# RWKV-7's block transfers between SBUF and DRAM scratch, issued from SP's queue

## The chip, the cores and the metric

One core of a Trainium2 chip runs the whole program. The metric is the device time of one execution in microseconds (us). The engines are named as in the profile: PE (TensorE), DVE (VectorE), ACT (ScalarE), POOL (GpSimd) and SP (SyncE). Any of ACT, POOL and SP can issue a DMA: the issue is an instruction in that engine's own program, and an engine runs its program in the order in which the framework's scheduler wrote it when the kernel was built.

## The reference

Two layers of a streaming-encoder trunk act on 512 frames of width 1024, all in fp32. Layer 0 normalises its input, projects it, and splits the columns between two mixers: HGRN2 (four heads, H0 to H3) and RWKV-7 (eight heads of width 64). Their outputs, ya and yb, are joined, projected by one output matrix, and added to x. A SwiGLU feed-forward block follows. Layer 1 does the same with S5 and mLSTM as mixers. A last normalisation closes it.

The part that matters here is RWKV-7's recurrence, which the reference runs frame by frame:

```python
def step(state, inp):
    r_t, w_t, k_t, v_t, a_t, b_t = inp
    sa = jnp.einsum("bhvk,bhk->bhv", state, a_t)
    state = (state * w_t[:, :, None, :] + sa[..., None] * b_t[:, :, None, :]
             + v_t[..., None] * k_t[:, :, None, :])
    return state, jnp.einsum("bhvk,bhk->bhv", state, r_t)
```

## The kernel before, in words

**Weights.** Every large product is made of three passes: weight and activation are each split into a high and a low part, and high by high, high by low and low by high are added up in PSUM. The weights stream in from DRAM one block after the other. `wissue` (L340) issues one block's load from SP into a tile `raw`, of which there are two. ACT casts it to `hi` (L375) and DVE or POOL subtracts to get `lo` (L376), 256 columns at a time. The rings of `hi` and `lo` hold two blocks, and the load of a block is written one block ahead of its use. PE's matmuls all stand at L292, and their results for dense products go to two PSUM tiles `d`. Small copies that any engine may do stand at L281, element by element products at L277, activations at L253.

**RWKV-7 by chunks.** The kernel takes 64 frames as a chunk, so that the recurrence becomes products of matrices and one triangular system for each chunk and head. Heads go in pairs P0 to P3, the sequence in two halves g = 0 and 1. One group (q, g) is two pairs and one half, so there are four groups. For each group there are three kinds of work:

- `rwp(q, g)`: gates and then `rw_prep` for both pairs. It builds the triangular matrix A in the tile `pb`. Its diagonal blocks of 32 by 32 are then written to DRAM scratch `scr_a`, with four DMAs for a pair (L952).
- `inv(q, g)`: `rw_inverse`, on POOL alone. It loads the blocks of both pairs back as `iw` and `iu` with one block to a partition (eight DMAs, L987 and L988), inverts them all at once in 30 steps (L992, L994), and stores the result to `scr_u` (four DMAs, L1000).
- `rwd(q, g)`: `rw_solve` for both pairs loads the inverted blocks into `ub` with four DMAs for a pair (L1010) and does four products with it. Then `rw_chain` carries the state through the four chunks: ACT and DVE copy a PSUM result to `sb` (L281), PE transposes it (L1059), and for pairs P0 and P1 SP stores the output to `scr_yb` (L1090).

There are 32 such DMAs at L952 in all and 32 at L1010, of 16 KB each.

**What sets the order.** The dense work F runs through the projections in the order L, P0, P1, H0, P2, P3, H1, H2, H3. A table, `prog`, weaves F with RWKV-7's groups: each stage takes F up to one label while it runs one or two group steps beside it. The last two stages are `inv(1,0)` and `rwp(1,1)` beside F up to H3, and `inv(1,1)` with `rwd(1,0)`. A head of HGRN2 (`hgrn`) ends with a store of its output `y` to `scr_ya` from SP (L837). After the last stage the pool of HGRN2's tiles is closed. `xtiles` (L520) then loads eight tiles x of the residual, 256 KB each, from ACT's queue, into memory that this pool held. `outa` reloads ya and yb as `yraw` from SP (L1174), splits them, multiplies five of the eight row blocks by the weights wO0a, and lets DVE add the PSUM result to x (L1183). It is woven with `rwd(1,1)`.

The scheduler weaves the program by its own estimate of when an instruction can start, so the order on every engine can shift when one instruction's engine is changed.

**The table that the change touches.** `dq(j)` gives the queue for each of four kinds of DMA:

```python
def dq(j):
    return {"s": nc.sync, "g": G, "a": S}[PRM["dq"][j]]

dq(0).dma_start(scr_a[...], pb[...])    # L952, in rw_prep
dq(1).dma_start(iw[w], ...)             # L987, and iu at L988, in rw_inverse
dq(2).dma_start(scr_u[...], iw[w])      # L1000, in rw_inverse
dq(3).dma_start(ub[...], scr_u[...])    # L1010, in rw_solve
```

In it `S` is ACT's queue (nc.scalar), `G` is POOL's (nc.gpsimd) and `nc.sync` is SP's.

Of the kernel before, what the change touches and what calls it, by code (L numbers as in the profile page):

```python
# [195 lines left out]
    return o  # L196


PRM = {'c': (0, 1, 2, 3), 'seq': ['L', 'P0', 'P1', 'H0', 'P2', 'P3', 'H1', 'H2', 'H3'], 'm': {'inv': 1.728, 'rwp': 1.6, 'rwd': 0.675}, 'prog': [[('F', 'P1')], [('rwp', 0, 0), ('F', 'H0')], [('inv', 0, 0), ('rwp', 0, 1), ('F', 'P2')], [('inv', 0, 1), ('rwd', 0, 0), ('F', 'H1')], [('rwd', 0, 1), ('rwp', 1, 0), ('F', 'H2')], [('inv', 1, 0), ('rwp', 1, 1), ('F', 'H3')], [('inv', 1, 1), ('rwd', 1, 0)]], 'e': 0.2, 'k': 8.0, 'dq': 'aggg', 'j': 0.9, 'eng': {('h8', 2): 'G', ('c5', 0, 0): 'S', 'h7': 'G', 'c7': 'S', ('p2', 3, 0): 'S', ('c1', 0, 0): 'S', ('c1', 1, 0): 'S', 'c6': 'V', 'c4': 'S', ('c1', 2, 0): 'V', 'h3': 'V', ('p14', 3, 0): 'V', ('h8', 1): 'G', ('c7', 1): 'V', ('c5', 1): 'V', 'h5': 'V', ('c8', 2): 'G', ('p2', 0): 'S', ('s4', 1, 0): 'S', 's2': 'S', 'c2': 'S', 'z1': 'G', 'z4': 'G', 'z6': 'G', ('z5', 0): 'V', ('a6', 3): 'G', 'p10': 'V', 'z9': 'V', 'p13': 'S', ('z2', 1): 'G', ('z0', 4): 'S', ('z1', 3): 'V', 'h13': 'V', ('a6', 2): 'G', ('z0', 1): 'G', ('h12', 1): 'V', ('n2', 2): 'V', ('p11', 1): 'S', ('a2', 2): 'V'}, 'pu': (2, 4, 5, 6, 7, 9, 12, 13, 36), 'i': 1.0, 'h': 0.7, 'f': 1.4, 'pr': {}}


@with_exitstack
def trunk(ctx: ExitStack, tc: tile.TileContext, A, out, dbg=None, start=0):
# [68 lines left out]
    def on(op, i, j, default="V"):  # L272
        e = PRM["eng"]
        return ENG[e.get((op, i, j)) or e.get((op, i)) or e.get(op, default)]
# [34 lines left out]
    if start < 1:  # L309
        for s in PRM["seq"]:  # L310
            nm, a, b = {"L": ("wB", 0, 1), "P": ("wB", 1, 3), "H": ("wA", 0, 4)}[s[0]]
# [16 lines left out]
    def onpool(unit, part):  # L328
        return unit in PRM["pu"] and part in PRM["c"]

# [55 lines left out]
    def defer(f):  # L386

        later.append(f)
        early[0] = PRM.get("d", 2)

# [264 lines left out]
    def layer0():  # L655
# [216 lines left out]
        def t2(name):  # L872
            return pl.tile([P, N2 + 4], F32, tag="t", name=name, bufs=PRM.get("t", 7))

# [17 lines left out]
        def dq(j):  # L892
            return {"s": nc.sync, "g": G, "a": S}[PRM["dq"][j]]

# [864 lines left out]
```

## Time and profile before

| what | value |
|---|---|
| time, median of 3 runs | 1449.44 us (1443.37 to 1450.04) |
| the profiled execution's own time | 1446.87 us |
| its span | 1445.1 us |
| mean granted clock of PE | 0.98 |
| busy: PE, DVE, ACT, POOL | 96%, 65%, 47%, 22% of the span |

The span is what the profile shows, and 1.8 us of the execution's time lie outside it. Layer 0's mixers and output projection fill the first 430 us of it or so; the two feed-forward blocks and layer 1's mixers come after. A row of a timeline gives the start (us from the span's start), the duration, the engine (a q behind the name stands for its instruction queue, where DMA issues are recorded), the line, the operation with out<-in, and x with a count where neighbours are joined. Square brackets hold the idle time of that engine ahead of the row and what ended it. A row of windows gives the stretch and its length, then the busy time (and instructions) of PE, PE's weight loads, DVE, ACT and POOL, then the granted clock of PE (1.00 is full), the busy share of the DMA engines and GB/s.

### The profile page before, as it was taken

To read this page: it belongs to the slowest core of one execution; us is meant where nothing else is said; L and a number is where in the kernel's file an instruction comes from. 1 tells how busy PE (TensorE), PEld (TensorE's weight loads), DVE (VectorE), ACT (ScalarE), POOL (GpSimd) and SP (SyncE) were. 2 spreads that over 40 slices of the span, in tenths; PEclk is the share of its full clock that TensorE was granted. 3 is DMA by queue.
4 is the path that set the end of the run, shared out by engine and by line. 5 is a ranking of instruction groups with operands and counts; after the bars stand their busy time and mean duration, and the time that the engine had idled before them with its cause. 6 is when DMAs were issued, how large, how long until landed. Compare 5 with 4: busy or idle time off the path is not lost.

```text
span 1445.1 us, 19973 instructions
## 1 busy us (share of the span) xinstructions
PE 1391.6 (96%) x6668; PEld 1131.5 (78%) x6668; DVE 935.9 (65%) x2041; ACT 680.1 (47%) x1594; POOL 320.6 (22%) x590
## 2 busy tenths in 40 slices
PE   7989999989999999999999899999999999999997
PEld 5878878768878788888888678776678888888886
DVE  7578579898688555554444678679775555554343
ACT  7554565655464333334333333577454434434332
POOL 5355640667131233200001442000020000000001
PEclk9988999999999999999999999999999999999999
DMA  5221321123232333333333833311133333333332
GB/s 186 90 54 46 80 73 52 44 62 117 71 103 89 110 106 106 97 110 104 119 113 110 213 103 92 115 44 37 48 106 102 89 101 101 89 103 95 91 109 70
DMA packets 52551, 135.50 MB, mean 94 GB/s; under 512 B 11280, under 2 KB 16912, under 8 KB 52192
## 3 DMA queue, kind: packets, MB, share of 16 engines
q1 hardware_dynamic: 38656, 116.86, 26.6%
q0 software_dynamic: 4432, 9.36, 2.8%
q10 hardware_dynamic: 9360, 8.00, 1.8%
q8 instruction: 53, 0.87, 0.2%
q14 instruction: 50, 0.41, 0.1%
HBM read 123.81 MB, written 10.39 MB: 93 GB/s over the span
## 4 chain that ended last, share of the span: by engine, by line
PE 81%; DVE 10%; ACT 3%; DMA 2%; issue 1%; POOL 1%; ACTq 0%; DVEq 0%; SPq 0%; POOLq 0%
PE d L292 67%; PE m L292 8%; PE r L292 5%; DVE lo L376 1%; DVE e L277 1%; DMA raw<-in_wV_dram 1%; DVE hl L467 1%; ACT s L253 1%; DVE ks L277 1%; DMA x<-in_xT_dram 1%; ACT hi L375 1%; DMA raw<-in_wA_dram 0%; DVE u L277 0%; POOL ks L277 0%; ACTq L952 0%
## 5 line engine op out<-in xcount | busy, mean ns | idle before, releaser
L375 ACT CAST hi<-raw 128x256 fp32r<-128x256 f32 (+1 forms) x809 | 317.4, 402 | 499.1 <-PE d L292 451.2
L376 DVE TENSOR_TENSOR lo<-raw,hi 128x256 fp32r<-128x256 f32 (+1 forms) x774 | 341.4, 452 | 284.1 <-ACT hi L375 279.7
L292 PE MATMUL d<-hh,hi 128*128 128x512 f32 x1088 | 435.3, 400 | 1.7 <-DVE g L1207 1.6
L292 PE MATMUL d<-hh,lo 128*128 128x512 f32 x1088 | 431.5, 397 | 0.1
L292 PE MATMUL d<-hl,hi 128*128 128x512 f32 x1088 | 429.7, 395 | 0.0
L292 PEld LDWEIGHTS d<-hh,hi 128*128 128x128 f32 x1088 | 207.0, 190 | 45.6 <-ACT hi L375 2.3
L292 PEld LDWEIGHTS d<-hh,lo 128*128 128x128 f32 x1088 | 206.7, 190 | 44.4 <-issue 1.7
L292 PEld LDWEIGHTS d<-hl,hi 128*128 128x128 f32 x1088 | 206.7, 190 | 42.9 <-issue 1.6
L292 PE MATMUL d<-ah,hi 128*128 128x512 f32 x330 | 128.4, 389 | 0.0
L292 PE MATMUL d<-al,hi 128*128 128x512 f32 x330 | 128.4, 389 | 0.0
L292 PE MATMUL d<-ah,lo 128*128 128x512 f32 x330 | 128.4, 389 | 0.0
L1728 POOL TENSOR_TENSOR x<-x,f 128x256 f32<-128x256 f32 x6 | 5.2, 889 | 358.8 <-issue 352.3
L292 PE MATMUL d<-ysp,hi 128*128 128x512 f32 x224 | 75.4, 412 | 3.4 <-DVE x L1183 1.9
L473 POOL TENSOR_TENSOR rstd<-rstd,sq 128x512 f32<-128x512 f32 x21 | 29.0, 1381 | 196.4 <-ACT sq L253 196.3
L292 PEld LDWEIGHTS d<-ah,hi 128*128 128x128 f32 x330 | 61.9, 188 | 12.9
L292 PEld LDWEIGHTS d<-ah,lo 128*128 128x128 f32 x330 | 61.9, 188 | 12.9
L292 PEld LDWEIGHTS d<-al,hi 128*128 128x128 f32 x330 | 61.9, 188 | 12.8
L292 PEld LDWEIGHTS d<-ysp,hi 128*128 128x128 f32 x224 | 42.3, 193 | 13.5 <-DVE x L1695 2.3
L992 POOL TENSOR_TENSOR ti<-iu,iw 128x60 f32<-128x60 f32 (+10 forms) x120 | 41.0, 342 | 21.0 <-DMA iu<-scr_a 9.3
L292 PE MATMUL d<-ysp,lo 128*128 128x512 f32 x112 | 45.5, 407 | 0.0
L1207 DVE TENSOR_TENSOR g<-d,g 128x512 f32<-128x512 f32 x42 | 29.0, 691 | 24.4 <-PE d L292 24.4
L1204 DVE TENSOR_TENSOR g<-d,rstd 128x512 f32<-128x512 f32 x42 | 29.0, 690 | 21.7 <-PE d L292 21.7
(491 smaller groups left out, 2048.1 us busy)
## 6 DMA issues: line engine op xcount, KB each, us to landing
raw<-in_wGU_dram SPq DMA_DIRECT2D x88, 512.0 KB, 3.6
raw<-in_wD_dram SPq DMA_DIRECT2D x32, 512.0 KB, 3.5
raw<-in_wA_dram SPq DMA_DIRECT2D x16, 512.0 KB, 3.6
raw<-in_wB_dram SPq DMA_DIRECT2D x13, 512.0 KB, 3.7
raw<-in_wD_dram SPq DMA_DIRECT2D x16, 384.0 KB, 3.1
raw<-in_wV_dram SPq DMA_DIRECT2D x6, 512.0 KB, 5.1
raw<-in_wQ_dram SPq DMA_DIRECT2D x6, 512.0 KB, 3.5
raw<-in_wK_dram SPq DMA_DIRECT2D x6, 512.0 KB, 3.8
```

Source lines behind the costliest of these rows:

```text
L253: a = S.activation(o, i, f, bias=bias, scale=scale)
L277: on(op, i, j).tensor_tensor(o, a, b, f)
L292: T.matmul(o, w, a, start=start, stop=stop)
L375: S.copy(h, src)
L376: eng.tensor_tensor(l, src, h.bitcast(F32), SUB)
L467: V.scalar_tensor_tensor(self.hl[:, k, :], x, pc(self.g, k), self.hh[:, k, :].bitcast(F32), MUL, SUB)
L473: self.eng.tensor_tensor(self.rstd, self.rstd, sq, ADD)
L992: G.tensor_tensor(t3, iu[:, j:j + 1, j + 1:].to_broadcast([P, m, n]), iw[:, 0:m, j:j + 1].to_broadcast([P, m, n]), MUL)
L1204: V.tensor_tensor(g1, pg, rstd, MUL)
L1207: V.tensor_tensor(g1, pu_, g1, MUL)
L1728: G.tensor_tensor(x[k][:, t], x[k][:, t], r_, MUL)
```

## The change

One string in the table of parameters is another. The rest of the line is as it was.

```diff
-PRM = { ... 'k': 8.0, 'dq': 'aggg', 'j': 0.9, ... }
+PRM = { ... 'k': 8.0, 'dq': 'sggs', 'j': 0.9, ... }
```

So the 32 writes of A's diagonal blocks (L952) are issued from SP and no longer from ACT, and the 32 loads of the inverted blocks (L1010) from SP and no longer from POOL. The loads of iw and iu and the stores to `scr_u` stay on POOL. What each DMA moves is the same.

The lists below are the engines' programs as built. Names carry a buffer number there, which the profile leaves out: `pb_254` and `pb_272` are the two pairs' tiles in half 0, `pb_263` and `pb_281` those in half 1, `ub_237` and `ub_239` the tiles of a group's first and second pair.

SP's program around the first group, from the weights of H0 on (wB are the weights of RWKV-7's projections, wA those of HGRN2's); the difference, with - for before and + for after:

```order
 L340 DMA raw<-in_wA_dram 128x1024 x4
-L340 DMA raw<-in_wB_dram 128x1024 x6
+L340 DMA raw<-in_wB_dram 128x1024 x3
+L952 DMA scr_a<-pb_254 32x4x32 x4
+L952 DMA scr_a<-pb_272 32x4x32 x4
+L340 DMA raw<-in_wB_dram 128x1024 x2
+L1010 DMA ub_237<-scr_u 32x4x32 x4
+L1010 DMA ub_239<-scr_u 32x4x32 x4
 L837 DMA scr_ya<-y 128x512
-L340 DMA raw<-in_wA_dram 128x1024 x5
+L340 DMA raw<-in_wB_dram 128x1024
```

The eight block writes and the eight block loads now stand among the weight loads, and the sixth of these wB loads stands behind the block loads and behind H0's store to `scr_ya`.

SP's program at the end of layer 0's mixers, before. The store to `scr_ya` is H3's, and the wO0a loads are the weights of `outa`:

```order
L1174 DMA yraw<-scr_yb 128x512 x2
L340 DMA raw<-in_wO0a_dram 128x640
L837 DMA scr_ya<-y 128x512
L340 DMA raw<-in_wO0a_dram 128x640
L1174 DMA yraw<-scr_ya 128x512
L340 DMA raw<-in_wO0a_dram 128x640 x2
```

The same place after the change. `ub_237` and `ub_239` belong to the last group, `rwd(1,1)`:

```order
L1174 DMA yraw<-scr_yb 128x512 x2
L340 DMA raw<-in_wO0a_dram 128x640
L1010 DMA ub_237<-scr_u 32x4x32 x4
L837 DMA scr_ya<-y 128x512
L1010 DMA ub_239<-scr_u 32x4x32 x4
L1174 DMA yraw<-scr_ya 128x512
L340 DMA raw<-in_wO0a_dram 128x640 x3
```

Four block loads of the last group stand ahead of H3's store to `scr_ya`, and four ahead of the reload of it and of the next weights.

ACT's program around the start of H3's gates (the activations at L253 with `s`), before:

```order
L375 CAST hi<-raw 128x128
L952 DMA scr_a<-pb_263 32x4x32 x4
L952 DMA scr_a<-pb_281 32x4x32 x4
L253 ACTIVATE s_3518<-u_3319 128x512
L733 COPY vt<-m 128x512
```

The same place after the change:

```order
L375 CAST hi<-raw 128x128
L375 CAST hi<-raw 128x256
L281 COPY y_265<-r 64x4x64 x2
L281 COPY ek<-r 64x256 x2
L375 CAST hi<-raw 128x256
L253 ACTIVATE s_3518<-u_3319 128x512
L253 ACTIVATE s_3519<-u_3395 128x512
```

The eight issues are gone from ACT's program, and the copies of the last `rw_prep` (`y`, `ek`) stand ahead of H3's activations; before they stood behind them.

More of the change, by code (lines that the diff above doesn't have):

```diff
@@ L196, in _layout @@
     return o
-PRM = {'c': (0, 1, 2, 3), 'seq': ['L', 'P0', 'P1', 'H0', 'P2', 'P3', 'H1', 'H2', 'H3'], 'm': {'inv': 1.728, 'rwp': 1.6, 'rwd': 0.675}, 'prog': [[('F', 'P1')], [('rwp', 0, 0), ('F', 'H0')], [('inv', 0, 0), ('rwp', 0, 1), ('F', 'P2')], [('inv', 0, 1), ('rwd', 0, 0), ('F', 'H1')], [('rwd', 0, 1), ('rwp', 1, 0), ('F', 'H2')], [('inv', 1, 0), ('rwp', 1, 1), ('F', 'H3')], [('inv', 1, 1), ('rwd', 1, 0)]], 'e': 0.2, 'k': 8.0, 'dq': 'aggg', 'j': 0.9, 'eng': {('h8', 2): 'G', ('c5', 0, 0): 'S', 'h7': 'G', 'c7': 'S', ('p2', 3, 0): 'S', ('c1', 0, 0): 'S', ('c1', 1, 0): 'S', 'c6': 'V', 'c4': 'S', ('c1', 2, 0): 'V', 'h3': 'V', ('p14', 3, 0): 'V', ('h8', 1): 'G', ('c7', 1): 'V', ('c5', 1): 'V', 'h5': 'V', ('c8', 2): 'G', ('p2', 0): 'S', ('s4', 1, 0): 'S', 's2': 'S', 'c2': 'S', 'z1': 'G', 'z4': 'G', 'z6': 'G', ('z5', 0): 'V', ('a6', 3): 'G', 'p10': 'V', 'z9': 'V', 'p13': 'S', ('z2', 1): 'G', ('z0', 4): 'S', ('z1', 3): 'V', 'h13': 'V', ('a6', 2): 'G', ('z0', 1): 'G', ('h12', 1): 'V', ('n2', 2): 'V', ('p11', 1): 'S', ('a2', 2): 'V'}, 'pu': (2, 4, 5, 6, 7, 9, 12, 13, 36), 'i': 1.0, 'h': 0.7, 'f': 1.4, 'pr': {}}
+PRM = {'c': (0, 1, 2, 3), 'seq': ['L', 'P0', 'P1', 'H0', 'P2', 'P3', 'H1', 'H2', 'H3'], 'm': {'inv': 1.728, 'rwp': 1.6, 'rwd': 0.675}, 'prog': [[('F', 'P1')], [('rwp', 0, 0), ('F', 'H0')], [('inv', 0, 0), ('rwp', 0, 1), ('F', 'P2')], [('inv', 0, 1), ('rwd', 0, 0), ('F', 'H1')], [('rwd', 0, 1), ('rwp', 1, 0), ('F', 'H2')], [('inv', 1, 0), ('rwp', 1, 1), ('F', 'H3')], [('inv', 1, 1), ('rwd', 1, 0)]], 'e': 0.2, 'k': 8.0, 'dq': 'sggs', 'j': 0.9, 'eng': {('h8', 2): 'G', ('c5', 0, 0): 'S', 'h7': 'G', 'c7': 'S', ('p2', 3, 0): 'S', ('c1', 0, 0): 'S', ('c1', 1, 0): 'S', 'c6': 'V', 'c4': 'S', ('c1', 2, 0): 'V', 'h3': 'V', ('p14', 3, 0): 'V', ('h8', 1): 'G', ('c7', 1): 'V', ('c5', 1): 'V', 'h5': 'V', ('c8', 2): 'G', ('p2', 0): 'S', ('s4', 1, 0): 'S', 's2': 'S', 'c2': 'S', 'z1': 'G', 'z4': 'G', 'z6': 'G', ('z5', 0): 'V', ('a6', 3): 'G', 'p10': 'V', 'z9': 'V', 'p13': 'S', ('z2', 1): 'G', ('z0', 4): 'S', ('z1', 3): 'V', 'h13': 'V', ('a6', 2): 'G', ('z0', 1): 'G', ('h12', 1): 'V', ('n2', 2): 'V', ('p11', 1): 'S', ('a2', 2): 'V'}, 'pu': (2, 4, 5, 6, 7, 9, 12, 13, 36), 'i': 1.0, 'h': 0.7, 'f': 1.4, 'pr': {}}
 @with_exitstack
```

## The prediction

> **What bounds the kernel now.** I read the page first, then windows of the two parts of the span, then the timelines of PE, ACT, POOL and SP around each place where the order of the DMAs changes. The page:
>
> ```profile
> span 1445.1 us, 19973 instructions
> PE 1391.6 (96%) x6668; PEld 1131.5 (78%) x6668; DVE 935.9 (65%) x2041; ACT 680.1 (47%) x1594; POOL 320.6 (22%) x590
> PEclk9988999999999999999999999999999999999999
> ```
>
> PE bounds the kernel; no other engine comes near. Time can only be won or lost where PE idles or runs at a lower clock. The windows, ahead of 430 us (layer 0's mixers) and behind it:
>
> ```profile
> 0.00:430.00 430.00, 403.00 (x2213) 329.20 (x2214) 330.18 (x777) 248.52 (x620) 198.77 (x433) 0.96 0.27 81
> 430.00:1445.10 1015.10, 988.63 (x4456) 802.28 (x4455) 605.76 (x1265) 431.56 (x974) 121.78 (x157) 0.99 0.33 99
> ```
>
> Every changed DMA lies in the first part, where PE idles 27.0 us. That is all that better cover could save there, beside the loss of clock. The second part has no block DMA and should only be shifted. The changed queue matters most at the end of the mixers, where the timelines of POOL, SP, ACT, DVE and PE read:
>
> ```profile
> 331.18 0.23 POOL L992 TENSOR_TENSOR ti<-iu,iw 128x30 f32<-128x30 f32 x1 [2.57 <-issue]
> 357.23 1.74 POOL L1000 DMA_DIRECT2D scr_u<-iw  x3
> 359.41 0.56 POOL L1000 DMA_DIRECT2D scr_u<-iw  x1 [0.29 <-POOL iw L999]
> 364.12 4.35 POOL L1010 DMA_DIRECT2D ub<-scr_u  x8 [4.15 <-PE r L292]
> ...
> 352.08 0.78 DVE L836 SCALAR_TENSOR_TENSOR y<-y,par,u 128x512 f32<-128x512 f32 x1
> 352.88 0.32 SPq L837 DMA_DIRECT2D scr_ya<-y  x1
> 354.96 0.88 ACTq L520 DMA_DIRECT2D x<-in_xT_dram  x2
> 356.62 0.21 ACT L281 COPY sb<-r 64x64 f32<-64x64 f32 x1 [1.44 <-DVE sb L281]
> 359.91 0.69 DVE L1183 TENSOR_TENSOR x<-x,d 128x512 f32<-128x512 f32 x1 [1.97 <-DMA x<-in_xT_dram]
> 360.65 0.73 PE L292 MATMUL d<-ysp,hi 128*128 128x512 f32 x2 [1.87 <-DVE x L1183]
> ```
>
> Two strands run side by side. One is POOL's last inversion, whose four stores are issued by 359.41 + 0.56 = 359.97. The other is H3: its y is ready at 352.86, SP stores it at once, and ACT issues the first two x loads 2.08 us after that store. The x tiles lie in memory that HGRN2's pool held, so they wait for its last reader, this store. The load ends DVE's wait at 359.91, DVE's add frees a PSUM tile, and PE, which had run out, goes on. From the store on this strand has no slack.
>
> **The change part by part.**
>
> *H3's store held behind the block loads.* In the new SP order the four loads of `ub_237` stand ahead of this store. They cannot go before the last inversion has landed, and SP waits in order, so the store is no longer issued at 352.88. The landing, at two earlier groups:
>
> ```profile
> 127.28 0.56 POOL L1000 DMA_DIRECT2D scr_u<-iw  x1 [0.29 <-POOL iw L999]
> 129.73 4.35 POOL L1010 DMA_DIRECT2D ub<-scr_u  x8 [1.90 <-DMA scr_u<-iw]
> 304.26 0.56 POOL L1000 DMA_DIRECT2D scr_u<-iw  x1 [0.29 <-POOL iw L999]
> 306.68 4.38 POOL L1010 DMA_DIRECT2D ub<-scr_u  x8 [1.86 <-DMA scr_u<-iw]
> 81.81 4.14 ACTq L952 DMA_DIRECT2D scr_a<-pb  x8
> ```
>
> There the loads go 1.90 and 1.86 us behind the last store's issue. At the last group it was 4.15, with the x loads in flight; its releaser by name is a matmul, so I take the 4.15 as an upper bound for the landing. After the change the x loads come later and cannot disturb it: I take 1.88. Four issues cost 2.07 by ACT's row (8 in 4.14), where DMAs of the same shape go out; SP's 0.32 for one store would make 1.28, POOL's 4.38 for 8 makes 2.19. The store then goes at 359.97 + 1.88 + 2.07 = 363.92, 11.0 later than 352.88. Bounds: 359.97 + 1.86 + 1.28 = 363.11 gives 10.2, and 359.97 + 4.15 + 2.19 = 366.31 gives 13.4.
>
> Who waits for that: SP holds behind it H3's reload and the next wO0a loads. ACT holds the x loads, and behind them the `sb` copies (356.62 is one), without which PE's transposes of the chain cannot run; the casts of the next weights too. DVE holds the add, and PE the dense products, with both PSUM tiles taken. So both of PE's sources dry up, and the 11.0 goes on the path whole. **+11.0.**
>
> *The clock.* [...] The places in the trace, as windows and PE rows:
>
> ```profile
> 319.00:326.00 7.00, 3.25 (x13) 2.46 (x14) 6.00 (x13) 6.83 (x17) 5.54 (x9) 0.52 0.37 98
> 356.00:361.00 5.00, 3.13 (x23) 2.57 (x22) 2.39 (x7) 0.62 (x3) 3.28 (x11) 1.00 0.96 345
> 322.24 1.06 PE L959 MATMUL r<-con,raw 128*64 128x128 f32 x4 [4.59 <-ACT y L281]
> ```
>
> After 4.59 us idle the clock was 0.52 through a stretch of 7.0, which holds 3.25 of work that would take about half of that: some 1.6 lost. After 1.87 idle at 360.65 it stayed 1.00. An idle time of 11 is longer than both. The lost time lies between 0 and the 3.4 that half speed would cost if all 7.0 were work. **+2**, near the case seen. [...]
>
> *POOL freed of 32 issues, ACT of 32.* POOL's come after an inversion, when its next one has not begun. What matters is whether the last inversion starts earlier. Its loads:
>
> ```profile
> 313.10 4.05 ACTq L952 DMA_DIRECT2D scr_a<-pb  x8
> 317.20 0.63 ACT L253 ACTIVATE s<-u 128x512 f32<-128x512 f32 x1 [8.56 <-DVE vf L725]
> 318.99 0.59 POOL L987 DMA_DIRECT2D iw<-scr_a  x1 [7.93 <-DMA scr_a<-pb]
> 323.04 0.77 POOL L277 TENSOR_TENSOR e<-c 128x256 f32<-128x256 f32 x1 [0.74 <-DVE u L277]
> 325.51 1.44 POOL L277 TENSOR_TENSOR e<-c 128x256 f32<-128x256 f32 x2 [0.65 <-PE m L292]
> 326.89 0.51 POOL L988 DMA_DIRECT2D iu<-scr_a  x1
> ```
>
> ACT held its eight writes from 313.10 to 317.15, waiting for `pb`, and H3's sigmoid chain started behind them. That chain feeds the `e` products on POOL, which stand among the eight loads and ended them at 327.40. In the new order ACT is free of the 4.05, but puts the last `rw_prep`'s copies ahead of the sigmoid chain. So PE's gap of 4.59 at 322.24 should shrink by about 2, while the `e` products come about when they did. The writes themselves go out when `pb` is ready, from whichever queue. Since a later hold ends when POOL's chain says so, what PE gains at 322 it waits for at 357. One thing is added: the new POOL program, as built, has four of the eight loads, not three, behind the last two `e`: +0.51, by the row at 326.89. **+0.5**, with bounds of 4.05 earlier (ACT's whole time) and as much later, if the reordering delays `e`.
>
> *The other places.* SP's wB and wA loads stand behind block loads at the other groups. They come up to 10 us later (third rival), and I count **0**: what hides it is that ACT's casts, the first users of a load, wait for PE and not for DMA (rows there).
>
> Sum: 11.0 + 2 + 0.5 + 0 = +13.5. Against the profiled execution's 1446.87 us that is 1460.4; against the mean of its time and the three others, 1447.43, it is 1460.9. I take **1461.0**, 0.8% above the median of 1449.44. By the bounds: 10.2 - 4.05 + 0 = +6.2 gives 1453.0, and 13.4 + 3.4 + 0.5 + 4.05 = +21.4 gives 1468.3.
>
> **The rivals.**
>
> *Faster, since ACT is free.* If the sigmoid chain starts at 313 and with it POOL's loads come together, the gap of 4.59 goes, and with it up to 3.4 of lost clock: -8, or 1441.4 from the median. For the hold to vanish too, the last inversion must land before 352.9, so 9 us earlier than 361.85. POOL idled 7.93 before 318.99, but that was for `pb`, which no queue makes earlier; and `e` stays among the loads. Chance 0.08.
>
> *No change.* The same DMAs move the same bytes, and the store's delay is hidden behind other PE work: 1447.4 to 1449.4. For it: PE is 96% busy over the span, so there is work elsewhere. Against it: PE ran out at 358.78 already, and the row at 360.65 names x. In the stretch 356 to 361 PE had 3.13 of 5.00 to do. Chance 0.12. [...]
>
> *Slower still: late weights.* The rows of SP, and what ACT's casts waited for between 60 and 350 us (total us, times, longest):
>
> ```profile
> 121.20 7.03 SPq L340 DMA_DIRECT2D raw<-in_wB_dram  x2
> 136.26 0.33 SPq L837 DMA_DIRECT2D scr_ya<-y  x1
> 289.96 10.85 SPq L340 DMA_DIRECT2D raw<-in_wO0a_dram  x2
> 306.09 0.33 SPq L837 DMA_DIRECT2D scr_ya<-y  x1
> ...
>   ACT hi L375 <- PE d L292: 44.4, 41, 4.4
>   ACT hi L375 <- DMA raw<-in_wA_dram: 0.4, 1, 0.4
> ```
>
> The second wB load of 121.20 (issued by 128.23) now stands behind the first group's `ub` and H0's store, so at 136.6 or later, 8.4 late. The second wO0a load (by 300.81) stands behind the third group's `ub`, so at 306.68 + 4.14 = 310.8, 10.0 late. If one of them is not covered, PE pays some 5 to 9 more: about 1468. Against it: 44.4 us of waiting for PE in 41 waits, against 0.4 for a DMA, so a block lies ready long before use, and a later one eats that first. Chance 0.10.
>
> **How the numbers follow.** Forecast 0.70, faster 0.08, no change 0.12, slower still 0.10. Half a per cent, 7.2 us, is about what a measurement of this kernel can tell from no change, so "same" ends at 1456.7. Of the forecast's own range, 1453.0 to 1468.3, about a tenth (0.07) lies under that. So faster 0.08, same 0.12 + 0.07 = 0.19, slower 0.63 + 0.10 = 0.73. The range 1447.0 to 1469.0 takes in the forecast, the second rival, and half of the third; it leaves out the first, which with the other half is 0.13, and what is unforeseen.
>
> **What would show it.** Right, step by step: H3's `scr_ya` store near 364 instead of 352.88, ahead of it SP waiting for `scr_u`; the first x load near 366; DVE's first add waiting 10 us or more for x; PE idle 9 to 11 us in all between 355 and 373, with a half clock behind it; the part after the mixers as long as before (1015 us). Wrong if the last inversion is done before H3's y, or PE has work through the hold, or if PE waits on raw near 135 or 310.

## The result, and the profile after

The changed kernel takes 1463.28 us (median of 4 runs, 1462.3 to 1467.47), beside 1447.96 us for the kernel before in the runs that were compared with it. The ratio is 1.0105, with a 95% interval of 1.008 to 1.013: about 15 us slower. The page of the profile after:

```profile
span 1461.2 us, 19990 instructions
PE 1400.6 (96%) x6668; PEld 1137.9 (78%) x6668; DVE 936.9 (64%) x2041; ACT 681.3 (47%) x1594; POOL 306.6 (21%) x558
PEclk9989999999899999999999999999999999999998
```

The busy shares hardly differ from before. POOL has 14 us less to do, which bought nothing. Windows of the kernel after, split where the mixers end (15 us later than the split that the prediction used):

```profile
0.00:445.00 445.00, 409.81 (x2222) 333.64 (x2223) 331.92 (x778) 251.78 (x624) 184.32 (x401) 0.95 0.28 79
445.00:1461.00 1016.00, 990.78 (x4447) 804.25 (x4446) 604.95 (x1263) 429.54 (x971) 122.24 (x157) 0.98 0.34 99
```

PE's idle time in the mixers went from 27.0 to 445.00 - 409.81 = 35.2 us. By this split the part behind them is as long as it was, 1016.00 us beside 1015.10. The end of the mixers, in the timelines of POOL, SP, ACT, DVE and PE after the change:

```profile
360.95 1.74 POOL L1000 DMA_DIRECT2D scr_u<-iw  x3
363.13 0.56 POOL L1000 DMA_DIRECT2D scr_u<-iw  x1 [0.29 <-POOL iw L999]
...
365.10 1.74 SPq L1010 DMA_DIRECT2D ub<-scr_u  x4
366.88 0.43 SPq L837 DMA_DIRECT2D scr_ya<-y  x1
367.41 1.82 SPq L1010 DMA_DIRECT2D ub<-scr_u  x4
...
358.50 0.74 ACT L281 COPY sb<-r 64x64 f32<-64x64 f32 x3 [2.09 <-PE r L292]
369.10 0.88 ACTq L520 DMA_DIRECT2D x<-in_xT_dram  x2
370.02 0.21 ACT L281 COPY sb<-r 64x64 f32<-64x64 f32 x1 [10.78 <-issue]
...
356.39 0.75 DVE L836 SCALAR_TENSOR_TENSOR y<-y,par,u 128x512 f32<-128x512 f32 x1
372.28 0.69 DVE L1183 TENSOR_TENSOR x<-x,d 128x512 f32<-128x512 f32 x1 [1.14 <-DMA x<-in_xT_dram]
437.15 0.67 DVE L1246 TENSOR_TENSOR x<-x,d 128x512 f32<-128x512 f32 x1
...
370.28 0.47 PE L1059 MATMUL r<-con,sb 128*128 128x128 f32 x1 [8.78 <-ACT sb L281]
```

H3's y is ready at 357.14 and its store goes at 366.88, behind four block loads that had waited for the last inversion. ACT sits 10.78 us at the first x load; the profile names no releaser there. The next `sb` copy stands behind that load, and PE waits 8.78 us for the copy. The first window below is the hold: PE, DVE and ACT stand still, and POOL is busy for 2.35 us, mostly with its stores. The second is the stretch behind it, in which the clock is still low:

```profile
361.00:370.00 9.00, 0.49 (x2) 0.30 (x2) 0.12 (x1) 0.00 (x0) 2.35 (x6) 0.63 0.26 58
370.00:376.00 6.00, 5.72 (x32) 5.23 (x32) 2.64 (x7) 1.24 (x6) 0.00 (x0) 0.70 0.98 330
```

To measure the hold in any kernel I take the stretch from the start of H3's last product (DVE, L836) to the start of DVE's last add to x (L1246). Before, that add stands here:

```profile
424.51 0.68 DVE L1246 TENSOR_TENSOR x<-x,d 128x512 f32<-128x512 f32 x1
```

So the stretch was 424.51 - 352.08 = 72.4 us before and is 437.15 - 356.39 = 80.8 after: **+8.3 us**. What is left of the 15 us lies elsewhere. In these two profiles, whose spans differ by 16.1 us, 4.3 lie ahead of y and 3.5 behind that last add, where the change moves nothing; in the second profile of the change, below, those two are 5.1 and -0.3. The part behind the mixers varies by that much from execution to execution.

### The profile page after: what moved, and what is told of

Its sections match the earlier page's. It is cut to its first block, busy times and chain, and to the rows that moved or that the text cites. A ratio compares the mean times of both kernels' runs of the same rounds, so it can differ in the third digit from the quotient of the medians.

```text
span 1461.2 us, 19990 instructions
## 1 busy us (share of the span) xinstructions
PE 1400.6 (96%) x6668; PEld 1137.9 (78%) x6668; DVE 936.9 (64%) x2041; ACT 681.3 (47%) x1594; POOL 306.6 (21%) x558
## 4 chain that ended last, share of the span: by engine, by line
PE 68%; DVE 4%; POOL 2%; issue 1%; ACT 1%; DMA 0%; SPq 0%; ACTq 0%; DVEq 0%; POOLq 0%
PE d L292 60%; PE m L292 7%; PE r L292 2%; POOL iw L994 1%; DVE lo L376 1%; POOL ti L992 1%; DVE hl L467 1%; DVE ks L277 0%; POOL ks L277 0%; DVE hst L277 0%; DMA raw<-in_wO0b_dram 0%; DVE x L1726 0%; PE m L1365 0%; DMA scr_ya<-y 0%; PE r L1059 0%
## 5 line engine op out<-in xcount | busy, mean ns | idle before, releaser
L292 PEld LDWEIGHTS d<-al,hi 128*128 128x128 f32 x330 | 61.9, 188 | 12.8
L292 PEld LDWEIGHTS d<-ysp,hi 128*128 128x128 f32 x224 | 41.9, 191 | 13.8 <-DVE x L1246 2.4
L994 POOL TENSOR_TENSOR iw<-iw,ti 128x60 f32<-128x60 f32 (+10 forms) x120 | 44.3, 369 | 9.4
```

The source lines that it names most:

```text
L292: T.matmul(o, w, a, start=start, stop=stop)
L994: G.tensor_tensor(iw[:, 0:m, j + 1:], iw[:, 0:m, j + 1:], t3, ADD)
```

## The experiments

The theory at this point: the block loads of the last group hold H3's store, and by it the x loads. The rivals: the writes or the new order of ACT make the loss; or loads on SP cost at every group. Each kernel below is `before.py` or `after.py` with the edit shown. "Stretch" is the one defined above.

| kernel | time against before (95%) | stretch |
|---|---|---|
| before | | 72.4 |
| the change | 1.0105 (1.008 to 1.013) | 80.8 |
| the change, again | 1.0124 (1.0099 to 1.0149) | 81.0 |
| writes only | 0.9973 (0.9949 to 0.9997) | 72.5 |
| writes only, again | 1.0005 (0.9985 to 1.0024) | 72.9 |
| loads only | 1.0104 (1.0079 to 1.0128) | 83.2 |
| last group's loads only | 1.0069 (1.0049 to 1.0089) | 81.8 |
| the change, last group's loads on POOL | 1.0045 (1.0025 to 1.0065) | 72.7 |
| the change, H3's store on ACT | 1.0062 (1.0046 to 1.0079) | 79.9 |
| one load only | 1.0066 (1.0041 to 1.0091) | 80.0 |
| one load only, H3's store on ACT | 1.0029 (1.0011 to 1.0046) | 73.0 |
| third group's loads only | 1.0036 (1.0019 to 1.0052) | 73.0 |
| the same, one weight load on ACT | 1.0019 (1.0001 to 1.0037) | 72.0 |
| the change, last group on POOL, two weight loads on ACT | 1.0042 (1.0024 to 1.006) | 72.9 |

**The two parts alone.** First only the writes:

```diff
-'dq': 'aggg'
+'dq': 'sggg'
```

> Only A's block writes go to SP; the loads of the inverted blocks stay on POOL, so nothing that waits for an inversion stands ahead of H3's store on SP. Theory (held store): H3's store to scr_ya goes as soon as y is ready, the idle time of 8.78 us near 370 is gone, and only what the changed kernel had lost before its hold stays: y there was 4.3 us later than before, so +2 to +6 us against before. Rival (SP's writes among the weight loads, or the new order of ACT as a whole, cost the time): +10 us or more, with PE waiting for raw or for ACT's copies.

The hold is gone: the stretch is 72.5. The time was outside what was expected, on the better side: 0.27% faster, where +2 to +6 us were forecast. The same program once more:

> The writes alone on SP a second time, for another profile and more runs: the first profile was of the slowest of its twelve runs (1456.9 of 1438.4 to 1456.9). Expected: 2 to 6 us faster than before in the median, and in a profile with no such clock loss near 220 to 233 H3's y at 352 to 354.

This time no difference could be measured (1.0005), where 2 to 6 us were expected. The two together say that the writes on SP neither help nor harm by more than a few tenths of a per cent. The second profile puts H3's y at 347.29, the first at 357.81, though the program is the same. That is why positions ahead of y are not compared below from single profiles, and the stretch is.

Then only the loads:

```diff
-'dq': 'aggg'
+'dq': 'aggs'
```

> Only the loads of the inverted blocks go to SP; A's writes stay on ACT, and ACT's order around 313 to 325 is that of before. All eight loads of the last group now stand ahead of H3's store, not four. Theory: the store goes after the last inversion has landed and eight issues, 359.97 + 1.41 + 8 x 0.45 = 365.0 where before had 352.88, so +12 us (10 to 15), all of it in one idle time of PE near 360 to 370. Rival (the writes and ACT's order make the loss): within 4 us of before.

1.0104, as much as the whole change. The loss belongs to the loads. The stretch is longer than with the change (83.2), and here eight loads, not four, stand ahead of the store. The expectation was wrong in one point: it wanted all of it in one idle time of PE. There are two, 9.33 us at 371.59 and 10.94 us at 325.45, where before had 4.59.

**Which loads.** Only the last group's eight on SP:

```diff
-dq(3).dma_start(ub[...], ...)
+(nc.sync if g == 1 and p > 1 else G).dma_start(ub[...], ...)
```

> The kernel before, with only the eight loads of the last group issued from SP: one of the four groups, none of the writes. Theory: as with all loads on SP, the store is held to about 365.0, +12 us (10 to 15), though 24 of the 32 loads and all the writes are where they were. Rival (the loss is spread over the groups, or comes from the order of the other engines): +1 to +4 us.

SP, ACT and PE in this kernel:

```profile
361.67 3.64 SPq L1010 DMA_DIRECT2D ub<-scr_u  x8
365.40 0.38 SPq L837 DMA_DIRECT2D scr_ya<-y  x1
...
367.97 0.21 ACT L281 COPY sb<-r 64x64 f32<-64x64 f32 x1 [9.93 <-DMA scr_ya<-y]
...
368.23 0.48 PE L1059 MATMUL r<-con,sb 128*128 128x128 f32 x1 [8.13 <-ACT sb L281]
```

The store at 365.40 is where the theory had it (365.0), and ACT's wait names it. The time is 10 us up (0.69%), at the low edge of what was expected. So a quarter of the loads makes more than half of the loss, but not all of it. The other three quarters, in the changed kernel with the last group taken back:

```diff
 'dq': 'sggs'
-dq(3).dma_start(ub[...], ...)
+(G if g == 1 and p > 1 else nc.sync).dma_start(ub[...], ...)
```

> The whole change, except that the eight loads of the last group (half 1, pairs P2 and P3) are issued from POOL again. All 32 writes and 24 of the 32 loads are on SP. Theory: only the last group's loads hold the end, so the idle time near 370 is gone and the time is that of the writes alone, from 6 us faster to 3 us slower than before. Rival (loads on SP cost at all groups): +8 us or more stay.

The hold goes, with a stretch of 72.7. But 0.45% (0.25 to 0.65), 6.5 us, stay, nearer to the rival's 8 than to the theory's range of up to 3. The two parts add up: 0.69 + 0.45 = 1.14%, between the two measurements of the whole change (1.05 and 1.24).

**What holds the x loads.** If it is H3's store alone, another queue for it should free the end:

```diff
 'dq': 'sggs'
-nc.sync.dma_start(scr_ya[h], y)
+(S if h == 3 else nc.sync).dma_start(scr_ya[h], y)
```

> The whole change, but H3's store to scr_ya is issued from ACT, so that it stands behind no block load; H0 to H2 still store from SP. Theory: the hold goes, x loads follow the store by 2 us as before, and +2 to +6 us stay, as with the writes alone. Rival (it is not the store: weights or yraw behind the block loads on SP hold the end): the idle time near 370 stays, +12 us or more.

It did not. The time is 0.62% up, 9 us, between the theory's +2 to +6 and the rival's +12. The store goes at 354.32, 0.8 us after y's start, and ACT still stands, in SP's and ACT's timelines:

```profile
362.22 3.64 SPq L1010 DMA_DIRECT2D ub<-scr_u  x8
...
354.32 0.34 ACTq L837 DMA_DIRECT2D scr_ya<-y  x1
364.77 0.85 ACTq L520 DMA_DIRECT2D x<-in_xT_dram  x2
365.66 0.21 ACT L281 COPY sb<-r 64x64 f32<-64x64 f32 x1 [9.29 <-DMA ub<-scr_u]
```

The releaser is now the block load itself, with which the x load shares no data. The program as built tells why. In it, each DMA of SP and of ACT signals on one of eight semaphores, DMAHW0 to DMAHW7, so a load on ACT can share one with a load on SP. The first x load's waits, in this kernel and before:

```
L520 DMA x_4037<-in_xT_dram 128x512 [waits DMAHW6_49,DMAHW4_49,Activation_49]
L520 DMA x_4037<-in_xT_dram 128x512 [waits DMAHW2_49,Activation_49]
```

In this kernel the eight block loads use seven of the eight semaphores and H3's store the other one (DMAHW6). DMAHW4, on which the first x load waits, was last used by the third block load. So here the x loads on ACT wait for block loads (the 9.29 us above), though the store went 10.45 us ahead of them. Two kernels separate the two ways. One single block load on SP, ahead of H3's store:

```diff
-dq(3).dma_start(ub[...], ...)
+(nc.sync if (g, p, h, b) == (1, 3, 1, 1) else G).dma_start(ub[...], ...)
```

> The kernel before, with one single load on SP: the last of the last group's eight. H3's store stands behind it on SP and behind nothing else that waits. Theory (held store): one load holds it as eight do, but for the time of their issues: the store near 362, first x load near 364, idle time of PE of 5 us or more, +5 to +9 us. Second theory (x loads wait for the loads themselves by the eight DMA semaphores that SP and ACT share): with one load only one of them is taken, by the fifth x load, so without the store's part little would be left: +1 to +3 us.

and one single load with the store on ACT (the load is pair P2's first here, and the store's edit is that above):

> The kernel before, with one single load of the last group on SP and H3's store issued from ACT. The first four x loads now wait for nothing of an inversion; the program shows that the fifth waits for the semaphore that the one load uses, though it has no data to do with it. Theory of the shared semaphores: the first four x loads follow the store near 355 to 358, DVE's first adds come as before, the fifth x load goes only after the block load has landed, near 363, and ACT's copies stand behind it: +2 to +5 us, in a gap that begins later than before. If the store alone were the holder: no x load waits for a block load, and the time is that of before within 2 us.

SP and ACT in the first of the two:

```profile
360.40 0.32 SPq L1010 DMA_DIRECT2D ub<-scr_u  x1
360.82 0.38 SPq L837 DMA_DIRECT2D scr_ya<-y  x1
...
363.97 0.21 ACT L281 COPY sb<-r 64x64 f32<-64x64 f32 x1 [7.73 <-DMA scr_ya<-y]
```

And in the second, with the store on ACT:

```profile
364.14 0.32 SPq L1010 DMA_DIRECT2D ub<-scr_u  x1
...
362.65 4.82 ACTq L520 DMA_DIRECT2D x<-in_xT_dram  x2
367.51 0.21 ACT L281 COPY sb<-r 64x64 f32<-64x64 f32 x1 [4.93 <-DMA ub<-scr_u]
```

With the store behind it, one load holds nearly as long as eight: the stretch is 80.0, the time 0.66% up (9.6 us; +5 to +9 was expected). With the store free, four x loads go at once and the fifth waits 4.93 us for a load that it has nothing to do with. It is the one whose wait in the program is for that load's semaphore. PE idles 1.49 us there and not 5.70, and the stretch is 73.0. The time is 0.29% up (4.2 us), as that theory had it, but the stretch accounts for only 0.6 of it. Both ways exist, then. Either alone is enough to hold the end: without the store's part the changed kernel's stretch is 79.9, and one load ahead of the store, in the kernel before, gives 80.0. SP's own next loads are not what holds it: in the second kernel H3's reload and a weight load also stood behind the block load and went 4.7 us later against y than before, and the stretch stayed at 73.0.

**The other groups.** Where do the other 6 us go? PE's idle time and its mean granted clock between 60 and 350 us, beside the start of H3's last product, show why one profile can't tell:

| kernel | idle, us | clock | H3's y |
|---|---|---|---|
| writes only | 13.8 | 0.93 | 357.81 |
| writes only, again | 14.8 | 0.97 | 347.29 |
| the change | 16.0 | 0.95 | 356.39 |
| the change, again | 24.7 | 0.97 | 357.20 |
| the change, last group's loads on POOL | 22.6 | 0.98 | 354.28 |
| the change, H3's store on ACT | 22.4 | 0.98 | 353.53 |

The two profiles of the writes alone idle alike. Their clocks make 290 x (0.97 - 0.93) = 11.6 us by estimate, about the 10.5 that lie between their y. The pair with the same clock is "writes only, again" and "the change, again": there y is 9.9 us later, and PE idles 9.9 us more. In the other pair, with lower clocks, the loads add 2.2 us of idle time and y comes no later. The measured times say 6.5 us, with an interval from 3.6 to 9.4. PE's idle times in the second profile of the change, with ACT's cast and copy that stand ahead of the second of them, and what ACT's casts waited for (between 60 and 350 us):

```profile
143.89 1.06 PE L958 MATMUL r<-con,ar 128*64 128x128 f32 x4 [5.20 <-ACT y L281]
319.84 0.64 PE L958 MATMUL r<-con,ar 128*64 128x128 f32 x2 [6.48 <-ACT y L281]
326.55 0.56 PE L971 MATMUL r<-con,bb 128*128 128x128 f32 x3 [3.09 <-ACT y L281]
...
315.88 0.91 ACT L375 CAST hi<-raw 128x256 fp32r<-128x256 f32 x3 [15.58 <-DMA raw<-in_wO0a_dram]
319.05 0.73 ACT L281 COPY y<-r 64x256 f32<-64x256 f32 x2
...
ACT hi L375 <- DMA raw<-in_wO0a_dram: 17.5, 2, 15.6
ACT hi L375 <- DMA raw<-in_wB_dram: 11.6, 1, 11.6
```

Before, that table had 0.4 us for a DMA; with the writes alone no such wait was over 5.7. The weight load behind the block loads comes late. PE does not need that block yet, but its cast stands early in ACT's program, and the copies `y` of the last preparation stand behind it. At the third group all profiles with the writes and these loads on SP show it: PE waits 2.4 to 6.5 us at this L958, and with the writes alone 0.4 at most. The first profile of the change has the least of it:

```profile
313.76 0.37 SPq L340 DMA_DIRECT2D raw<-in_wO0a_dram  x1
...
317.33 0.91 ACT L375 CAST hi<-raw 128x256 fp32r<-128x256 f32 x3 [12.81 <-PE d L292]
...
319.89 0.41 PE L958 MATMUL r<-con,ar 128*64 128x128 f32 x2 [2.37 <-ACT y L281]
```

Its wait of 12.81 us bears PE's name, but the weight load was only issued at 313.76. At the first group the gap near 143 is there in three profiles (5.1 to 5.4 us) and not in this one. The solves did not get their blocks late: at the third group the block loads went 1.4 us behind the last store to `scr_u` in both profiles of the change, and 1.9 and 3.0 with the writes alone.

The third group alone, in the kernel before:

```diff
-dq(3).dma_start(ub[...], ...)
+(nc.sync if g == 0 and p > 1 else G).dma_start(ub[...], ...)
```

> The kernel before, with only the eight loads of the third group (half 0, pairs P2 and P3) on SP. The second load of wO0a stands behind them on SP; its cast stands early on ACT, ahead of A's writes, H3's sigmoid chain and the copies y that PE waits for near 322. Theory (late weights through ACT's order): the load goes near 311 where before had 300.48, ACT sits 10 us or more at the cast for raw, its writes and the sigmoid chain start 2 to 3 us later, PE's idle time at 322 grows from 4.6 to 7 or more, +3 to +7 us. If late weights are covered, as the prediction had it: within 2 us of before, and the gap at 4.6.

and with the late weight load (number 31, counted from 0) issued from ACT:

```diff
-nc.sync.dma_start(raw[:, :n], ...)
+(S if pos[1] == 31 else nc.sync).dma_start(raw[:, :n], ...)
```

> The same, with that one load of wO0a issued from ACT, so that it stands behind no block load; the order of ACT's other instructions is the same. Theory: the cast has its data when its turn comes, the idle time at 322 is back at about 4.6, and the time is within 2 us of before, though the eight loads still are on SP. If it was the loads on SP themselves (or the pairs' solves coming later): as the kernel before this one, +3 to +7 us.

ACT and PE in the first of these:

```profile
313.57 0.41 ACT L375 CAST hi<-raw 128x256 fp32r<-128x256 f32 x1 [10.24 <-DMA raw<-in_wO0a_dram]
...
322.69 1.06 PE L959 MATMUL r<-con,raw 128*64 128x128 f32 x4 [4.68 <-ACT y L281]
```

The cast waits 10.24 us as foreseen, but PE's gap stays at 4.68. In this order of ACT the wait lies where ACT had nothing to do before (8.56 us until `vf`), and the sigmoid chain stands next. So here the late weight cost PE nothing. The kernel with its load on ACT had the wait down to 2.92 us and PE's gap at 5.36, no shorter. The 0.36% and 0.19% that were measured overlap in their intervals, and no wait in the profiles stands for them. But that is a matter of when the inversion ends and not of this order as such. "Loads only" has the same order of ACT; against this kernel its dense work was 3.6 us ahead (H2's y) and its block loads 1.8 behind, and there the late cast did reach PE:

```profile
315.21 0.40 ACT L375 CAST hi<-raw 128x256 fp32r<-128x256 f32 x1 [15.61 <-DMA raw<-in_wO0a_dram]
320.41 0.63 ACT L253 ACTIVATE s<-u 128x512 f32<-128x512 f32 x1 [4.30 <-DMA scr_a<-pb]
325.45 1.06 PE L959 MATMUL r<-con,raw 128*64 128x128 f32 x4 [10.94 <-ACT y L281]
```

Its sigmoid chain started at 320.41, where before had 317.20, and PE waited 10.94 us, where before had 4.59. In the changed order, where the copies stand right behind the cast, the cure was tried on both late loads:

```diff
 'dq': 'sggs'
-dq(3).dma_start(ub[...], ...)
+(G if g == 1 and p > 1 else nc.sync).dma_start(ub[...], ...)
-nc.sync.dma_start(raw[:, :n], ...)
+(S if pos[1] in (17, 31) else nc.sync).dma_start(raw[:, :n], ...)
```

> The kernel with the last group's loads on POOL (4.5 per mille slower than before, its hold at the end gone), with two weight loads issued from ACT: the wB load that stood behind the first group's block loads on SP and the wO0a load that stood behind the third's. Theory (in the order that ACT has when the writes are on SP, a cast that waits for a late weight keeps the copies y and ek from PE): ACT's waits for raw of 11.8 and 14.6 us go, PE's idle times of 5.4 at 143 and 4.25 at 317 with them, and the time is that of the writes alone, within 4 us of before, 5 to 8 us faster than with the two loads on SP. Rival (the rest comes from the pairs' solves, which get their blocks later from SP, or from the writes behind block loads): 5 to 8 us slower than before still.

No gain: 1.0042 beside 1.0045. SP, ACT and PE near the third group:

```profile
309.68 3.64 SPq L1010 DMA_DIRECT2D ub<-scr_u  x8
...
311.32 0.34 ACTq L340 DMA_DIRECT2D raw<-in_wO0a_dram  x1
314.41 0.91 ACT L375 CAST hi<-raw 128x256 fp32r<-128x256 f32 x3 [14.05 <-DMA raw<-in_wO0a_dram]
...
318.37 0.64 PE L958 MATMUL r<-con,ar 128*64 128x128 f32 x2 [4.97 <-ACT y L281]
```

The load on ACT went out only at 311.32, 1.64 us after the first block load was issued, and in the program it waits for DMAHW0, which that block load uses too. The cure ran into the second way of the hold, and the cast still waited 14.05 us. At 143 the gap is gone from this profile, but its clock was lower ahead of that place (0.89 between 60 and 135 us; 1.00 with the gap). The first profile of the change has no gap there either, with the load on SP and a clock of 0.91. So one profile doesn't show that the moved load did it.

**The change again**, for the second profile used above:

> The changed kernel again, for a second profile. Two profiles of the kernel with the writes alone differ by 10 us ahead of H3's y, with the same program, so what lies ahead of it is not to be read from one profile. Expected: +13 to +17 us; from the start of H3's last product y to the last of DVE's adds in the mixers 80 to 82 us again (72.4 before), wherever y comes.

1.0124, 18 us, just above the +13 to +17 expected; the stretch is 81.0, as expected.

## Why the prediction was right, and where its steps were not

- **The direction, the place and the main mechanism held.** The prediction had H3's store near 364 behind the four `ub_237` loads, the first x load near 366, and PE idle 9 to 11 us. Measured: 366.88 and 369.10, with y itself 4.3 us later than before, and 9.73 us of idle time between 355 and 373, 8.78 of them in one piece. DVE's first add names only 1.14 us of waiting for x, not the 10 foretold, though DVE was busy for 0.12 us of the hold. The last group alone on SP costs 0.69%, of 1.05 and 1.24 for the whole change.
- **The term "+11.0" was 8.3.** From the start of y the store waited 10.49 us and not 0.80, so 9.7 of the 11.0. Four issues took 1.78 us (365.10 to 366.88) for the 2.07 taken, the landing 1.41 (from 363.69) for the 1.88, and y stood 0.56 us nearer to the inversion's end. The path from the store to the first add then took 5.40 us, and before 7.03. Why it was 1.6 us shorter no run shows.
- **That the store is the holder was half of it.** The prediction saw one chain: store, x load, add. The x loads also wait for the block loads themselves, by the shared semaphores (9.29 us of ACT's time with the store on ACT). It changed little in the number, as either way holds the end alone. It decides what a cure must do: moving the store alone leaves 0.62%.
- **The clock's "+2" was about 0.** The clock did fall, to 0.63 in the window 361 to 370, and it was 0.70 from 370 to 376. But no run shows a loss of 2: the first add came 8.1 us late against y, and the last 8.3, so what lies behind the first add cost 0.2; in the second profile 0.7 (7.9 and 8.6). Most of the slow stretch lay ahead of the first add, which waited for x and not for PE, and PE was busy for only 0.49 us of the window 361 to 370.
- **The "+0.5" can't be checked.** It lies ahead of the hold, where two executions of one program differ by 10 us.
- **The step that failed is "The other places ... I count 0".** Its ground was that "ACT's casts, the first users of a load, wait for PE and not for DMA". That is a row of the kernel before, and it says nothing of a load that comes 10 us later. With the loads on SP the third group's cast waited 12.8 and 15.6 us in the two profiles of the change, and PE 2.4 and 6.5 us for the copies behind it. With the last group's loads back on POOL, the other 24 loads and the writes cost 0.45% (6.5 us). The third rival named the late weights and gave them 0.10; but it looked for PE waiting for the weights, where PE waits for copies that stand behind their casts on ACT.
- **The first rival and the second fell.** ACT without its eight issues did not start H3's sigmoid chain early (320.95 beside 317.20 before), and writes on SP gained at most 0.27%. The transfers are the same, but what stood behind them moved, and the change cost 1.05% and 1.24%; one load of 16 KB on SP alone (the kernel with one load) cost 0.66%.

The sum came out near by luck in part, because two errors went against each other: 13.5 forecast as 11.0 + 2 + 0.5 + 0, and some 15 measured, of them 8.3 at the end and about 6.5 at the other groups. What stays open is how those 6.5 come about in full. At the third group every profile with the changed order of ACT shows PE waiting for the copies behind the late cast. At the first only three of five do, those with a full clock ahead of it; that a slower PE leaves time for the late weight is likely, but no run shows it. And the kernel that should have cured both places did not get the third group's load out in time.

## What to carry to other kernels

A DMA that must wait for another engine's result belongs on a queue in which nothing urgent stands behind it; one such load ahead of H3's store cost 0.66% here. Before moving one, list what follows it on the new queue, and follow each of these to its first user in that engine's own order: a weight that nobody needs yet can still stop an engine if its cast stands early, as ACT here for 12.8 and 15.6 us. Look at the waits of the program as built too, since DMAs on different queues may be tied by the semaphores that they share, as the x load here that waited 4.93 us.

## What the runs showed of the hardware

- In this program as built, DMAs issued from SP and from ACT are tied by eight semaphores. An x load on ACT held it 4.93 us for a block load on SP with which it shares no data (the kernel with one load and the store on ACT).
- Issues of the same 16 KB block loads took less on SP than on POOL: 3.64 us for the last group's eight (0.45 each, in the kernel with them alone on SP) beside 4.35 (0.54, before).
- One program can reach the same instruction 10 us apart in two profiled executions (H3's y at 357.81 and 347.29), with PE idle for 13.8 and 14.8 us between 60 and 350 and a granted clock of 0.93 and 0.97 there, while a stretch of 72 us within it repeats to 0.4 us. Parts of a kernel should be compared by stretches between two of its own instructions.
